# Folding the squares of an attention norm in half before the product with ones

## The chip, the cores and the metric

The kernel runs on one NeuronCore of a Trainium2 chip. The metric is the time of one execution in microseconds (us) on the device. The engines are called as the profile calls them: PE (TensorE, matrix products), DVE (VectorE), ACT (ScalarE), POOL (GpSimd) and SP (SyncE, which issues most DMA transfers).

## What the kernel computes

One layer of a hybrid decoder, on x of 1024 positions by 1024 features in float32. Eight heads of differential attention and four heads of gated linear attention (GLA) read the same normed input, and their outputs go through one output projection.

```python
h = rms_norm(x, pre_g)
z = h @ w_in                          # split into qa, ka, va, ga, qb, kb, vb, gb, gk_low
oa = diff_attention(qa, ka, va, lam)  # 8 heads, 2 softmax maps each, v of 128 features
oa = rms_norm(oa, subln_g) * (1.0 - lam_init)   # over the 128 features of a head
oa = oa * silu(ga)
ob = rms_norm(gla_chunked(qb, kb, vb, log_a), gla_g) * silu(gb)
y = concatenate([oa, ob]) @ w_out
return x + rms_norm(y, post_g)
```

The change touches only the norm of `oa`: for each head and position, the mean of the squares of 128 features.

## The kernel before

**Stages.** The input projection and GLA take the first two thirds of the span. From about 655 us to 940 us of the profile the kernel runs attention, and beside it the part of the output projection whose inputs exist already. The end of the output projection and the last norm follow.

**Exact products.** PE multiplies in a rounded 32-bit type (fp32r). Operands that need more precision are split in a high part (an ACT copy that rounds) and a low part (a DVE subtraction of the rounded value from the full one), and products are made of both. Names that end in `_hi` and `_lo` are such pairs: `wt_hi`/`wt_lo` (transposed attention weights), `m_hi`/`m_lo` (mixed values, read back from DRAM as `m_raw`), `wo_hi`/`wo_lo` (output weights).

**The streams of the attention stage.** Three generators are interleaved by `merge`, which picks the stream whose clock is behind and advances that clock by the cost that the stream yields:

- `all_scores`: for each head, eight blocks of 128 queries, from block 7 (1024 keys) down to block 0. PE makes `sc`; DVE (L1167) masks and takes the row minimum; ACT (L1177) takes exp; then DVE's reciprocal (L1202), POOL's scaling of the second map, `p1` (L1203), and DVE's subtraction of the maps into `p0` (L1207).
- `all_values`: for each head, four pairs of query blocks. Each step (`turn`) transposes three or four 128x128 blocks of `p0` on PE (`wtr`), ACT copies them to `wt_hi` (L1244), DVE makes `wt_lo` (L1245), and PE multiplies with v into `po`. ACT copies `po` to the head's output `o` (L1272), 128 features on the partitions by 512 positions.
- `out_early`: partial products of the output projection, `ypart`, three products per 128 rows of `w_out`; ACT copies them out (`yst`). The `m_hi` and `m_lo` of the attention heads come from `mix_part` (L1360, L1361), whose `m_raw` is loaded from the DRAM tensor `mixd` once enough heads are stored there. `early_ends` goes on with this around the end of the last head; the products there are `yps`.

**The norm.** `attn_norm(h, half, o)` is a generator too, and runs once for each head and half of the positions, 16 times. `mingle` puts one of its steps behind each step of the value products: half 1 runs beside the values of half 0 of the same head, half 0 beside the first values of the next head. It squares `o` (`sq`, L1282), splits the squares in a high and a low part (`sq_hl`, L1284 on ACT and L1285 on DVE), and two steps later multiplies a 128x128 matrix of ones with both parts into one PSUM bank, `ms`. Each product sums over the partitions, so `ms` is the sum of squares on every partition. ACT then makes the inverse root (`r`, L1295 and L1296), DVE multiplies `o` with it (L1297), POOL multiplies the gate (L1299), and SP stores the result into `mixd` (L1301). Of the last head nothing is stored: `last_mix` keeps the product, and `last_part` (L1367, L1368) splits it for the last `yps`.

**Queues and banks.** PE's products keep the order in which the program issues them. On ACT, DVE, POOL and SP a scheduler orders the instructions when the program is built; on the chip each engine's queue then runs strictly in that order. `wtr` and `ms` take turns on two PSUM banks (the list `TR`, counted by `n_tr`), so each use waits until the use before the last has been read out. `sq` and `r` share one buffer, and there is one buffer of `sq_hl`.

Of the kernel before, what the change touches and what calls it, by code (L numbers as in the profile page):

```python
# [8 lines left out]
F32 = mybir.dt.float32  # L9
F32R = mybir.dt.float32r  # L10
AF = mybir.ActivationFunctionType
ALU = mybir.AluOpType
PSUM = bass.MemoryType.PSUM

P = 128
# [16 lines left out]
def hymba_kernel(  # L32
# [21 lines left out]
    act, dve, pool, pe, sp = nc.scalar, nc.vector, nc.gpsimd, nc.tensor, nc.sync  # L54

    def fp(t):
        return t.bitcast(F32)

    def cols(half):
        return slice(half * 512, half * 512 + 512)  # L60
# [8 lines left out]
    ones = const.tile([P, P], F32R, name="ones")  # L69
# [28 lines left out]
    def bank(i, shape, name):  # L98
        return psum.tile(shape, F32, tag=f"b{i}", name=name)
# [10 lines left out]
    def mm(*a, **k):  # L110
        tc.keep_in_program_order(pe.matmul(*a, **k))  # L111
# [637 lines left out]
    up, keep = ku[:, 0], fp(ku)[:, 1]  # L749
# [345 lines left out]
    smp = smp_cm.__enter__()  # L1095
# [179 lines left out]
    def attn_norm(h, half, o):  # L1275
        if h < DA_HEADS - 1:
            gate = smp.tile([P, 512], F32, tag="gate", name="gate", bufs=2)
        else:
            gate = kp.tile([P, 512], F32, tag=("q1", "k1")[half], name="gate")
        sp.dma_start(gate, g_d[h][:, cols(half)])  # L1280
        sq = smp.tile([P, 512], F32, tag="r", name="sq", bufs=1)
        act.activation(sq, o, AF.Square)  # L1282
        hl = smp.tile([P, 2, 512], F32R, tag="sq_hl", name="sq_hl", bufs=1)
        act.copy(hl[:, 0], sq)  # L1284
        dve.tensor_tensor(hl[:, 1], sq, fp(hl[:, 0]), ALU.subtract)  # L1285
        yield 0.0
        yield 0.0
        n_tr[0] += 1
        ms = bank(TR[n_tr[0] % 2], [P, 512], "ms")
        for i in range(2):  # L1290
            mm(ms, ones, hl[:, i], start=(i == 0), stop=(i == 1))
        if h == DA_HEADS - 1 and not half:
            opened[TR[n_tr[0] % 2]] = None
        r = smp.tile([P, 512], F32, tag="r", name="r", bufs=1)
        act.activation(r, ms, AF.Ln, bias=eps_t, scale=1.0 / P)  # L1295
        act.activation(r, r, AF.Exp, scale=-0.5)  # L1296
        dve.scalar_tensor_tensor(r, o, sub_g, r, ALU.mult, ALU.mult)  # L1297
        dst = o if h < DA_HEADS - 1 else gate
        pool.tensor_tensor(dst, r, gate, ALU.mult)  # L1299
        if h < DA_HEADS - 1:  # L1300
            sp.dma_start(mixd[h * P : (h + 1) * P, cols(half)], o)  # L1301
            stored.append(h)
        else:
            last_mix[half] = gate
        yield 0.0
# [13 lines left out]
    def all_values():  # L1319
        carry = iter(())  # L1320
        nxt = v_first
        for h in range(DA_HEADS):
            v = nxt
            o = [smp.tile([P, 512], F32, tag="o", name="o", bufs=3) for _ in range(2)]
            yield from mingle(values(h, 3, v, o[1]), carry)
            if h + 1 < DA_HEADS:
                nxt = load_v(h + 1)
            yield from values(h, 2, v, o[1])
            yield from mingle(
                chain(values(h, 1, v, o[0]), values(h, 0, v, o[0])), attn_norm(h, 1, o[1])  # L1330
            )
            carry = attn_norm(h, 0, o[0])
        last_part(ENDS[0], parts_d[ENDS[0]])
        yield next(carry)
        yield lambda: (ENDS[2], 0) in ps_d
        early_ends()
        yield from carry
# [309 lines left out]
```

## Time and profile before

| | |
|---|---|
| Time, median of 3 runs | 977.59 us (977.15 to 982.69) |
| The profiled execution | 977.73 us |
| Its span in the profile | 976.0 us, so 1.73 us lie around it |
| PE busy | 98% of the span, 4866 products |
| DVE, ACT, POOL busy | 76%, 61%, 22% |
| Granted TensorE clock | 0.998 on average |

A row of the timeline has the start, the duration (both in us), the engine, the line of the kernel, the operation, output and inputs by the program's names, the size, and the count. In brackets stands how long the engine sat idle before it and what ended that. Matmuls are pipelined, so the durations of neighbouring ones overlap, and what one costs PE is the distance from its start to the next start.

### The profile page before, as it was taken

Reading aid. Unit: us, or ns where it says so; the run is one execution under the profiler, and the core shown is the slowest. Engines: PE = TensorE matmul, PEld = TensorE weight load, DVE = VectorE, ACT = ScalarE, POOL = GpSimd, SP = SyncE. Lnnn points to the kernel's source line nnn. Section 1 sums busy time; section 2 is a strip of 40 time slices with the busy share of each in tenths; the row PEclk is TensorE's granted clock in tenths of the full one; section 3 lists DMA queues with packets and bytes.
Section 4 is the critical chain, followed back from the end, with each engine's and each line's share of the span. In section 5 each row is a group of like instructions: output and inputs, shape, how many; then the busy total and the mean of one; then the engine's idle time right before and its main releaser. Section 6 shows DMA issues by size and latency. Waiting matters only on the chain.

```text
span 976.0 us, 14803 instructions
## 1 busy us (share of the span) xinstructions
PE 956.0 (98%) x4866; PEld 806.1 (83%) x4866; DVE 738.7 (76%) x1450; ACT 590.9 (61%) x1152; POOL 211.5 (22%) x289
## 2 busy tenths in 40 slices
PE   6999999999999999999999999999999999999997
PEld 4888888878888888888888888788888888888875
DVE  6996476889889776778787766577787778887655
ACT  8641232347467467766677774357667667787764
POOL 5420100011211221112110000023232233443232
PEclk9999999999999999999999999999999999999999
DMA  8354643768865875899986569997575678995657
GB/s 306 99 152 153 212 134 98 217 174 270 265 240 194 268 250 192 265 280 304 315 278 183 180 204 346 376 337 233 164 252 185 189 267 246 331 262 104 194 157 156
DMA packets 144556, 220.37 MB, mean 226 GB/s; under 512 B 14704, under 2 KB 78704, under 8 KB 144384
## 3 DMA queue, kind: packets, MB, share of 16 engines
q1 hardware_dynamic: 130144, 175.38, 56.6%
q0 software_dynamic: 14336, 44.05, 15.1%
q8 instruction: 38, 0.62, 0.3%
q14 instruction: 38, 0.31, 0.1%
HBM read 133.93 MB, written 88.60 MB: 228 GB/s over the span
## 4 chain that ended last, share of the span: by engine, by line
PE 86%; DMA 6%; DVE 3%; ACT 3%; issue 1%; SPq 1%; DVEq 0%; POOL 0%; ACTq 0%
PE v L111 15%; PE x L111 15%; PE ypart L111 11%; PE y L111 10%; PE z L111 10%; PE sc L111 6%; PE po L111 5%; PE yps L111 4%; PE wtr L114 3%; PE gpo L111 2%; PE kv L111 1%; DMA m_raw<-mixd 1%; DMA m_lo<-mixe 1%; DMA mixd<-o 1%; DMA k_d<-qk_st 1%
## 5 line engine op out<-in xcount | busy, mean ns | idle before, releaser
L1177 ACT ACTIVATE p<-p,stt 128x896 f32<-128x896 f32 (+7 forms) x128 | 99.3, 777 | 46.7 <-DVE stt L1167 43.5
L335 DVE TENSOR_TENSOR w<-w_raw,w 128x512 fp32r<-128x512 f32 x134 | 91.9, 690 | 32.5 <-ACT w L333 32.1
L333 ACT CAST w<-w_raw 128x512 fp32r<-128x512 f32 x134 | 82.5, 620 | 42.9 <-PE y L111 19.9
L1203 POOL TENSOR_SCALAR p<-p,stt,lam 128x1024 f32<-128x1024 f32 (+3 forms) x64 | 55.7, 871 | 209.6 <-DVE stt L1202 203.9
L1167 DVE CUSTOM_DVE_ANT_0 p<-sc,maskt 128x512 f32<-128x512 f32 (+3 forms) x128 | 74.4, 585 | 33.2 <-PE sc L111 32.5
L111 PE MATMUL y<-h_hi,w 128*128 128x512 f32 x320 | 80.6, 394 | 0.0
L111 PE MATMUL x<-s_hi,w 128*128 128x512 f32 x320 | 80.5, 394 | 0.0
L111 PE MATMUL z<-s_hi,w 128*128 128x512 f32 x320 | 80.4, 393 | 0.0
L111 PE MATMUL ypart<-wo_hi,m_hi 128*128 128x512 f32 x192 | 79.5, 414 | 0.6 <-ACT yst L1384 0.5
L111 PE MATMUL v<-w,s_hi 128*128 128x512 f32 x256 | 79.0, 389 | 0.1
L111 PE MATMUL ypart<-wo_hi,m_lo 128*128 128x512 f32 x192 | 75.6, 394 | 0.7 <-DMA m_lo<-mixe 0.7
L111 PE MATMUL ypart<-wo_lo,m_hi 128*128 128x512 f32 x192 | 75.6, 394 | 0.5 <-DMA wo_lo<-wo_d 0.5
L488 ACT COPY s<-x 128x512 f32<-128x512 f32 x60 | 35.0, 584 | 65.2 <-PE x L111 65.0
L111 PE MATMUL sc<-k,q 128*128 128x512 f32 (+1 forms) x192 | 70.9, 372 | 0.4 <-DVE stt L1167 0.4
L111 PEld LDWEIGHTS z<-s_hi,w 128*128 128x128 f32 x320 | 59.1, 188 | 11.6
L111 PEld LDWEIGHTS x<-s_hi,w 128*128 128x128 f32 x320 | 59.1, 188 | 11.7
L111 PEld LDWEIGHTS y<-h_hi,w 128*128 128x128 f32 x320 | 59.0, 188 | 11.6
L111 PE MATMUL sc<-k,qs 128*128 128x512 f32 (+1 forms) x192 | 66.6, 349 | 0.0
L285 ACT CAST w<-w_block 128x1024 fp32r<-128x1024 f32 x24 | 25.0, 1051 | 65.3 <-PE v L111 42.3
L257 DVE TENSOR_TENSOR w_raw<-w_raw 128x512 f32<-128x512 f32 x80 | 55.3, 691 | 9.6 <-DMA w_raw<-in_w_in_dram 8.6
L111 PE MATMUL v<-w,h_hi 128*128 128x512 f32 x192 | 60.0, 400 | 0.4 <-ACT h_hi L582 0.4
L1207 DVE SCALAR_TENSOR_TENSOR p<-p,stt,p 128x1024 f32<-128x1024 f32 (+3 forms) x64 | 52.3, 819 | 6.7 <-POOL p L1203 6.5
(233 smaller groups left out, 2379.8 us busy)
## 6 DMA issues: line engine op xcount, KB each, us to landing
w_raw<-in_w_in_dram SPq DMA_DIRECT2D x40, 512.0 KB, 4.9
w_block<-in_w_in_dram SPq DMA_DIRECT2D x16, 512.0 KB, 4.4
wo_raw<-in_w_out_dram POOLq DMA_DIRECT2D x32, 256.0 KB, 4.2
wo_d<-wo_hi POOLq DMA_DIRECT2D x32, 256.0 KB, 4.5
wo_d<-wo_raw POOLq DMA_DIRECT2D x32, 256.0 KB, 5.0
qs<-q_d SPq DMA_DIRECT2D x32, 256.0 KB, 8.6
k<-k_d SPq DMA_DIRECT2D x16, 512.0 KB, 9.2
q<-q_d SPq DMA_DIRECT2D x16, 512.0 KB, 7.1
```

Source lines behind the costliest of these rows:

```text
L111: tc.keep_in_program_order(pe.matmul(*a, **k))
L114: tc.keep_in_program_order(pe.transpose(dst, src, ident))
L257: dve.tensor_tensor(dst, a, b, ALU.subtract)
L285: act.copy(w[0], src)
L333: act.copy(w[0], src)
L335: split_last[:] = [dve.tensor_tensor(w[1], src, fp(w[0]), ALU.subtract)]
L488: act.copy(b[k], ps)
L1167: ins = dve.tensor_tensor_reduce(p[:, a:e], sc[:, : e - a], maskt[:, NZ + P - (e - a) :] if last else maskt[:, : e - a], 1.0, 3e38 if i == ...
L1177: act.activation(p[:, :n], p[:, :n], AF.Exp, bias=st[:, m : m + 1], scale=-1.0, accum_out=st[:, 2 + m : 3 + m],)
L1203: pool.tensor_scalar(p1[:, :n], p1[:, :n], st[:, 5:6], lam, ALU.mult, ALU.mult)
L1207: dve.scalar_tensor_tensor(p0[:, :n], p0[:, :n], st[:, 4:5], p1[:, :n], ALU.mult, ALU.subtract)
```

## The change

The upper 64 partitions of the squares are copied down beside the lower 64 (`sq_up`, on ACT), and GpSimd adds the two (L1286 of the changed kernel). Two more yields follow. The high part of the folded squares then goes to partitions 0 to 63 of `sq_hl` (L1289) and the low part to partitions 64 to 127 (L1290), and after the two yields that were there before, one product with ones sums both parts. Lines from 1285 on move down by four (L1301 becomes L1305, L1360 becomes L1364).

```diff
         sq = smp.tile([P, 512], F32, tag="r", name="sq", bufs=1)
         act.activation(sq, o, AF.Square)
-        hl = smp.tile([P, 2, 512], F32R, tag="sq_hl", name="sq_hl", bufs=1)
-        act.copy(hl[:, 0], sq)
-        dve.tensor_tensor(hl[:, 1], sq, fp(hl[:, 0]), ALU.subtract)
+        hl = smp.tile([P, 512], F32R, tag="sq_hl", name="sq_hl", bufs=1)
+        up = smp.tile([P, 512], F32, tag="sq_up", name="sq_up", bufs=1)
+        act.copy(up[:64], sq[64:])
+        pool.tensor_tensor(sq[:64], sq[:64], up[:64], ALU.add)
+        yield 0.0
+        yield 0.0
+        act.copy(hl[:64], sq[:64])
+        dve.tensor_tensor(hl[64:], sq[:64], fp(hl[:64]), ALU.subtract)
         yield 0.0
         yield 0.0
         n_tr[0] += 1
         ms = bank(TR[n_tr[0] % 2], [P, 512], "ms")
-        for i in range(2):
-            mm(ms, ones, hl[:, i], start=(i == 0), stop=(i == 1))
+        mm(ms, ones, hl, start=True, stop=True)
```

On PE nothing but `ms` moves: 16 pairs of products go, and 16 single ones appear two value steps later. This is PE's order around the norm of half 0 of head 0; `wtr` are the transposes, first of four blocks (p_6292 and p_6197 are two query blocks' weights), then of three, and `sc` the scores of the next head.

```order
 L111 MATMUL ypart<-wo_lo,m_hi 128x512
-L111 MATMUL ms<-sq_hl,ones 128x512 x2
 L114 MATMUL wtr<-ident,p_6292 128x128
 L114 MATMUL wtr<-ident,p_6197 128x128
...
 L111 MATMUL sc<-k_5896,q_6191 128x384
 L111 MATMUL sc<-k_5896,qs_6193 128x384
+L111 MATMUL ms<-sq_hl,ones 128x512
 L114 MATMUL wtr<-ident,p_6292 128x128
 L114 MATMUL wtr<-ident,p_6197 128x128 x2
```

The product moved from the place ahead of the turn of four transposes to that directly ahead of the turn of three. Between the two turns there is now an `ms` on the rotating banks, and ahead of both there is none.

The other engines' orders move more. This is ACT in the kernel before, at the end of head 3 and the start of head 4, where `m_hi_8089` is the first high part that `out_early` makes from stored heads.

```order
L1244 CAST wt_hi_7901<-wtr_7896 128x512
L1296 ACTIVATE r_7890<-r_7890 128x512
L1177 ACTIVATE p1_7881,stt_7879<-p1_7881,stt_7879 128x512
L1360 CAST m_hi_8089<-m_raw_7787 128x512
L1244 CAST wt_hi_7944<-wtr_7940 128x384
L1177 ACTIVATE p0_7930,stt_7929<-p0_7930,stt_7929 128x384
```

In the changed kernel the same cast is called `m_hi_8105` and stands some 20 rows later, behind the exp of 1024 keys and both copies `yst`. The rows after it are the norm of half 1 of head 4.

```order
L1177 ACTIVATE p1_8054,stt_8052<-p1_8054,stt_8052 128x1024
L1388 COPY yst_8121<-ypart_7799 128x512
L1388 COPY yst_8124<-ypart_7800 128x512
L1364 CAST m_hi_8105<-m_raw_7801 128x512
L1364 CAST m_hi_8127<-m_raw_7801 128x512
L1272 COPY o_7826<-po_8026 128x256
L1282 ACTIVATE sq_8195<-o_7826 128x512
L1285 COPY sq_up_8198<-sq_8195 64x512
L1289 CAST sq_hl_8197<-sq_8195 64x512
L1177 ACTIVATE p0_8154,stt_8153<-p0_8154,stt_8153 128x896
L1244 CAST wt_hi_8174<-wtr_8169 128x512
L1244 CAST wt_hi_8205<-wtr_8201 128x384
```

Behind the norm's cast the exp of 896 keys now stands ahead of the two casts `wt_hi`; before, one of these casts stood ahead of that exp. DVE at the same place of the changed kernel has both low parts behind the subtraction of the maps of 1024 keys; the kernel before had the first of them, `m_lo_8090`, some 30 rows earlier.

```order
L1245 TENSOR_TENSOR wt_lo_8102<-wtr_8097,wt_hi_8101 128x384
L1202 RECIPROCAL stt_8052<-stt_8052 128x2
L1207 SCALAR_TENSOR_TENSOR p0_8053<-p0_8053,stt_8052,p1_8054 128x1024
L1365 TENSOR_TENSOR m_lo_8106<-m_raw_7801,m_hi_8105 128x512
L1365 TENSOR_TENSOR m_lo_8128<-m_raw_7801,m_hi_8127 128x512
L1167 ISA p0_8154,stt_8153<-sc_8156,maskt_5832 128x512
```

On SP the loads of `m_raw` for these parts move as well: from ahead of the loads of the output weights' second, third and fourth row group to behind them.

The third place is the end of attention, the norms of head 7, again on ACT; `gate` is the finished product of half 1, and `m_hi` its high part for the last `yps`. First the kernel before.

```order
L1295 ACTIVATE r_9581<-ms_9578,eps_t_64 128x512
L1272 COPY o_9247<-po_9538 128x256
L1296 ACTIVATE r_9581<-r_9581 128x512
L1244 CAST wt_hi_9601<-wtr_9597 128x384
L1272 COPY o_9247<-po_9596 128x256
L1367 CAST m_hi_9393<-gate_9551 128x128
L1282 ACTIVATE sq_9616<-o_9247 128x512
L1284 CAST sq_hl_9618<-sq_9616 128x512
```

And the changed kernel at the same place.

```order
L1244 CAST wt_hi_9624<-wtr_9620 128x384
L1299 ACTIVATE r_9630<-ms_9628,eps_t_64 128x512
L1300 ACTIVATE r_9630<-r_9630 128x512
L1272 COPY o_9273<-po_9619 128x256
L1371 CAST m_hi_9421<-gate_9579 128x128
L1282 ACTIVATE sq_9646<-o_9273 128x512
L1285 COPY sq_up_9649<-sq_9646 64x512
L1371 CAST m_hi_9421<-gate_9579 128x128
L1503 COPY yps_9663<-yp_9556 128x512
L1371 CAST m_hi_9548<-gate_9579 128x128
L1289 CAST sq_hl_9648<-sq_9646 64x512
```

Half 1's inverse root moved behind the last `wt_hi`, and half 0's squares now go through a copy, POOL's addition, and three instructions of other work before their cast.

## Prediction

> **What bounds the kernel now.** I read first the engines' share of the span, then the stages, then what PE waits for in the attention stage.
>
> ```profile
> PE 956.0 (98%) x4866; PEld 806.1 (83%) x4866; DVE 738.7 (76%) x1450; ACT 590.9 (61%) x1152; POOL 211.5 (22%) x289
> ```
>
> ```profile
> 700.00:740.00 40.00, 39.89 (x235) 34.67 (x234) 30.38 (x82) 26.84 (x60) 11.72 (x13) 1.00 0.64 211
> 900.00:940.00 40.00, 38.63 (x216) 32.59 (x216) 22.11 (x61) 27.94 (x66) 9.83 (x12) 1.00 0.57 164
> ```
>
> ```profile
> PE po L111 <- ACT wt_hi L1244: 0.6, 1, 0.6
> PE ypart L111 <- ACT yst L1384: 0.5, 1, 0.5
> PE wtr L114 <- ACT r L1295: 0.4, 1, 0.4
> ```
>
> The second view has, for each stretch, its length and then the busy time of PE, its weight loads, DVE, ACT and POOL. PE leaves 0.11 us of 40 free at 700 to 740 while DVE has 10 us, ACT 13 and POOL 28 to spare. The third view lists the largest waits of PE between 655 and 976 us. The time is therefore PE's sum of products plus a handful of waits of half a microsecond. A product less is worth its whole price; a wait that appears on PE costs its whole length, however idle the engine behind it is on average. So the question is not whether ACT and POOL have time for the fold, but whether anything in PE's fixed order now comes late.
>
> **What goes.** Sixteen products with ones. At head 0's half 1 the pair stands in the stream like this:
>
> ```profile
> 705.65 0.63 PE L111 MATMUL ms<-sq_hl,ones 128*128 128x512 f32 x2
> 706.12 0.57 PE L111 MATMUL po<-wt_hi,v 128*128 128x256 f32 x4
> ```
>
> From the start of the pair to the next start are 0.47 us, so one product is 0.235 us, and 16 are **-3.8 us** (0.4%). That is all the change can give, and it is already less than the 1% that a measurement of this kernel can tell from no change.
>
> **What is added.** The price of each operation:
>
> ```profile
> L1284 ACT CAST sq_hl<-sq x16: 619/620/624, 662.0 to 934.0; 128x512 fp32r<-128x512 f32 x16
> L1285 DVE TENSOR_TENSOR sq_hl<-sq,sq_hl x16: 679/686/767, 663.8 to 934.6; 128x512 fp32r<-128x512 f32 x16
> L971 ACT COPY sq<-sq x8: 618/619/620, 374.7 to 574.2; 64x512 f32<-64x512 f32 x8
> L972 DVE TENSOR_TENSOR sq<-sq x8: 675/684/685, 375.4 to 574.9; 64x512 f32<-64x512 f32 x8
> L1299 POOL TENSOR_TENSOR o<-r,gate x14: 1282/1300/2131, 670.9 to 913.6; 128x512 f32<-128x512 f32 x14
> ```
>
> GLA's norm (L971, L972) makes the same fold and shows that 64 partitions cost what 128 cost: 619 against 620 ns on ACT, 684 against 686 on DVE. So the cast and the subtraction become no shorter, and each norm adds 0.62 us on ACT for the copy and an addition on POOL. POOL's addition of 64 partitions isn't in the trace. Its bounds are half of L1299 (0.65) and L1299's longest (2.13); I take the median, 1.30, since the other two engines show no gain from fewer partitions. From squares to `ms` the chain grows from 0.62 + 0.69 to 0.62 + 1.30 + 0.62 + 0.69, that is by 1.9 us and two handovers. Two value steps later is 3.4 us at the next place shown (718.12 to 721.5), so in most places the chain is covered; on the engines' totals (16 × 0.62 on ACT, 16 × 1.30 on POOL, over 280 us) it would be free. [...]
>
> **What is moved**, in order of time. Places where PE's order meets something late:
>
> *Half 0 of heads 0 to 3.* The product now stands directly ahead of the turn of three transposes, on the bank between the two turns' own.
>
> ```profile
> 718.12 0.62 PE L111 MATMUL ms<-sq_hl,ones 128*128 128x512 f32 x2
> 721.09 0.68 DVE L1245 TENSOR_TENSOR wt_lo<-wtr,wt_hi 128x512 fp32r<-128x512 f32 x1
> 721.94 0.49 PE L114 MATMUL wtr<-ident,p 128*128 128x128 f32 x3
> ```
>
> Before, the turn of three took the bank of `ms`, long read out. Now it takes the bank of the turn of four, free only when `wt_lo` ends, at 721.77. PE, without the pair, arrives with the single product at 721.47 and at the transposes at 721.7. That is no slack at all, with a POOL addition ahead of this block's scaling that pushes DVE's work on. I take 0.2 us for each of the four (0 to 0.7): **+0.8**.
>
> *Site A, 809 to 814 us.* The first `m_hi` and `m_lo` from stored heads are needed at 811.19 and 811.52. Before, they were made 12 us ahead. After, their loads are queued on SP behind three loads of output weights, and both casts stand on ACT behind the two copies `yst`, both subtractions on DVE behind L1207 of 1024 keys.
>
> ```profile
> 798.75 0.62 ACT L1360 CAST m_hi<-m_raw 128x512 fp32r<-128x512 f32 x1 [2.26 <-issue]
> 799.40 0.69 DVE L1361 TENSOR_TENSOR m_lo<-m_raw,m_hi 128x512 fp32r<-128x512 f32 x1 [1.87 <-ACT m_hi L1360]
> ...
> 809.42 1.15 ACT L1177 ACTIVATE p<-p,stt 128x1024 f32<-128x1024 f32 x1
> 810.57 1.05 ACT L1384 COPY yst<-ypart 128x512 f32<-128x512 f32 x2
> 810.96 1.20 POOL L1203 TENSOR_SCALAR p<-p,stt,lam 128x1024 f32<-128x1024 f32 x1 [4.81 <-DVE stt L1202]
> 811.19 0.50 PE L111 MATMUL ypart<-wo_hi,m_hi 128*128 128x512 f32 x1 [0.45 <-ACT yst L1384]
> 811.52 0.39 PE L111 MATMUL ypart<-wo_hi,m_lo 128*128 128x512 f32 x1
> 812.19 1.28 DVE L1207 SCALAR_TENSOR_TENSOR p<-p,stt,p 128x1024 f32<-128x1024 f32 x1 [1.33 <-POOL p L1203]
> ```
>
> Exp, scaling and L1207 all hang on scores that PE made before this point, so PE's wait doesn't delay them: L1207 ends at 813.47, `m_lo` 0.69 later at 814.16. PE wanted it at 811.52: **+2.6** (1.9 if DVE's chain runs 0.7 earlier against PE than it did, 3.8 with an `m_lo` as slow as the 1.91 us shown under the rivals). It is the surest of the stalls.
>
> *Right behind it*, ACT has head 4's squares, copy and cast, the cast waiting for POOL in place, and then the exp of 896 keys ahead of `wt_hi`:
>
> ```profile
> 814.82 0.59 ACT L1244 CAST wt_hi<-wtr 128x512 fp32r<-128x512 f32 x1 [0.31 <-PE wtr L114]
> 815.86 1.05 ACT L1177 ACTIVATE p<-p,stt 128x896 f32<-128x896 f32 x1 [0.46 <-DVE stt L1167]
> 817.16 0.63 PE L111 MATMUL po<-wt_hi,v 128*128 128x256 f32 x4
> ```
>
> Shifted by 2.6, `po` is due at 819.8. The copy of `o` can begin at 815.4; then 0.37, 0.63, 0.62, POOL 1.30, the cast 0.62 and the exp 1.24 with its read, so `wt_hi` runs from about 820.2 to 820.8: **+1.0** (0 to 1.6).
>
> *Half 0 of head 4.* POOL's addition is ahead of its scaling of 640 keys, and DVE makes `sq_hl`'s low part behind L1207 and behind the scores of 384 keys.
>
> ```profile
> 831.86 0.87 POOL L1203 TENSOR_SCALAR p<-p,stt,lam 128x640 f32<-128x640 f32 x1 [0.59 <-DVE stt L1202]
> 835.51 0.54 DVE L1167 CUSTOM_DVE_ANT_0 p<-sc,maskt 128x384 f32<-128x384 f32 x1
> 835.76 0.49 PE L114 MATMUL wtr<-ident,p 128*128 128x128 f32 x3
> ```
>
> The addition takes POOL until about 833.0, L1207 then ends at 834.8, L1167 at 836.05, the subtraction at 836.7; PE wants `ms` at 835.5. **+1.2** (0 to 1.6). Half 0 of head 5 has the same pattern with other sizes; I take less than half, **+0.5** (0 to 0.8).
>
> *Stores of head 6.* The last heads' parts go through DRAM.
>
> ```profile
> 900.40 0.37 SPq L1301 DMA_DIRECT2D mixd<-o  x1
> 903.72 0.90 SPq L1348 DMA_DIRECT2D m_raw<-mixd  x2
> 909.26 0.93 ACT L1469 CAST m_hi<-m_raw 128x384 fp32r<-128x384 f32 x2 [2.50 <-DMA m_raw<-mixd]
> ```
>
> ACT already waits 2.50 us for them. The norm is two steps later, so I put the store 1.7 us later and `m_raw` with it; the changed order gives ACT about 1 us of other work first: **+0.7** (0 to 1.7).
>
> *The tail.*
>
> ```profile
> 931.58 0.68 PE L111 MATMUL po<-wt_hi,v 128*128 128x256 f32 x4 [0.57 <-ACT wt_hi L1244]
> 931.80 1.29 POOL L1299 TENSOR_TENSOR gate<-r,gate 128x512 f32<-128x512 f32 x1 [10.32 <-PE wtr L114]
> 933.13 0.30 ACT L1367 CAST m_hi<-gate 128x128 fp32r<-128x128 f32 x1
> 937.56 0.62 PE L111 MATMUL ms<-sq_hl,ones 128*128 128x512 f32 x2
> ```
>
> Half 1's product now fills the wait at 931.58, but its inverse root comes behind the last `wt_hi`, so POOL's gate ends at about 934.5 and not 933.1, and ACT waits for it ahead of half 0's squares. From there: 0.29, squares until 935.5, copy 936.1, POOL 937.4, cast 938.0, subtraction 938.7. PE's last `ms` is ready at 938.7 instead of 937.56, and nothing else is left to do: **+1.4** together with the two products already counted as saved (0 to 1.9).
>
> **Sum.** 0.8 + 2.6 + 1.0 + 1.2 + 0.5 + 0.7 + 1.4 = 8.2, less 3.8: +4.4 us on the profiled execution's 977.73 (span 976.0 and 1.73 around it), 982.1; its time is within 0.2 us of the median, so **982**. All low ends give 977.7 - 3.8 + 1.9 = 975.8, all high ends 988.1.
>
> **Rivals.**
> - *Nothing waits.* The 16 products go and the scheduler's order is slack enough everywhere: 977.7 - 3.8 = 973.9, faster. For it: the averages, DVE 76%. Against: site A is read off the order and L1207's row.
> - *Only site A waits*, and PE's stall there lets the other engines run ahead so that the later places are covered: 977.7 - 3.8 + 3.6 = 977.5. For it: before, the view of PE's waits lists no more than five in 320 us. Against: the tail has nothing to run ahead of.
> - *POOL's addition is slow and everything compounds*: slower. This pair shows what POOL and DVE do to each other:
>
> ```profile
> 824.56 1.67 POOL L1299 TENSOR_TENSOR o<-r,gate 128x512 f32<-128x512 f32 x1
> 824.87 1.91 DVE L1361 TENSOR_TENSOR m_lo<-m_raw,m_hi 128x512 fp32r<-128x512 f32 x1 [0.89 <-ACT m_hi L1360]
> ```
>
>  Side by side they take 1.67 and 1.91 us, against 1.30 and 0.69 apart. At 2.1 us each addition would lengthen four exposed chains (behind site A, heads 4 and 5, tail) by 0.8 and the four early turns of three by as much: 982.1 + 8 × 0.8 = 988.5. It decides from about 1.7 us in the median. [...]
>
> **Chances.** The forecast (979.5 to 985) 0.48; only site A (976.5 to 979.5) 0.2; nothing waits 0.12; slow additions (985 to 991) 0.2. Range 975 to 988, which leaves out most of the third and a third of the last. Slower by over 1% is 987.4 and more, half of the last case: 0.1. Faster by over 1% would need 9.8 us, and only 3.8 are there: 0.01. Within: 0.89.
>
> **What would show it.** In the changed profile PE should list new waits: `ypart` on DVE's `m_lo` of over 2 us near 808 to 815, `po` on `wt_hi` of about 1 behind it, `ms` on `sq_hl` at head 4's half 0 and in the tail, `wtr` on `wt_lo` four times; 16 single `ms`; POOL's L1286 near 1.3 us. I am wrong if the wait at site A is under 1.5 us, if L1286 takes under 1 or over 1.7 us, or if the store of head 6 isn't later.

## The result and the profile after

| | before | changed |
|---|---|---|
| Median | 979.54 us (977.15 to 982.69, 6 runs) | 989.15 us (987.77 to 991.15, 6 runs) |
| Ratio | 1 | 1.0098, 95% interval 1.0072 to 1.0123 |
| Profiled execution, span | 977.73, 976.0 us | 988.76, 987.0 us |

The change makes the kernel about 9.6 us slower. The forecast was 982, that is 4.4 us slower, and the range ended at 988: the sign was as forecast, the size was too small, and the time lies outside the range.

PE does 16 products less and is busy for a smaller share of a longer span:

```profile
span 987.0 us, 14802 instructions
...
PE 957.7 (97%) x4850; PEld 805.5 (82%) x4850; DVE 746.2 (76%) x1450; ACT 599.8 (61%) x1168; POOL 232.5 (24%) x305
```

PE's waits from 655 us on, five of 0.2 to 0.6 us before, are now 19 in eleven groups; the largest groups (total, times, longest):

```profile
PE ms L111 <- DVE sq_hl L1290: 3.0, 3, 1.4
PE ypart L111 <- ACT m_hi L1364: 2.7, 1, 2.7
PE po L111 <- DVE wt_lo L1245: 2.0, 3, 1.2
PE sc L111 <- DVE stt L1167: 1.5, 2, 1.0
PE wtr L114 <- DVE wt_lo L1245: 0.9, 3, 0.4
PE yps L111 <- DVE m_lo L1372: 0.7, 1, 0.7
```

All eleven add up to 12.5 us against 2.1 before, so they more than eat the 3.8 us that the products give. To see where, I compared the two traces place by place. PE's order is the same but for `ms`, so each turn of transposes can be paired with the same turn before; the difference of their starts grows by what the stretch in between lost. The columns end at the turns that start, before the change, at 808.1, 816.1, 828.1, 853.7, 891.3 and 920.6 us, the last at the last product. They begin at 664.3, where the difference is -1.5 us in the changed kernel's profile and between -1.5 and +5.2 in all others: that much the earlier stages vary between profiled executions, whatever the kernel, and it is taken off.

| us against before | heads 0-3 | site A | behind it | head 4 half 0 | head 5 | head 6 | tail | sum | time, ratio |
|---|---|---|---|---|---|---|---|---|---|
| changed kernel | 0.1 | 5.7 | 1.2 | 1.8 | 1.0 | 1.4 | 1.3 | 12.5 | 1.0098 |
| yields only | -1.1 | 0.3 | 0.0 | -0.1 | 0.3 | 2.9 | 0.4 | 2.7 | 1.0031 |
| fold, no yields | -2.6 | -0.2 | 0.2 | 4.1 | 3.9 | -1.0 | 1.2 | 5.5 | 1.0079 |
| fold on DVE | -2.9 | 2.5 | 1.5 | 1.7 | 0.7 | 1.6 | 0.7 | 5.8 | 1.0078 |
| m_raw first | 0.2 | -0.7 | -0.1 | 5.4 | 1.0 | 2.4 | 1.2 | 9.3 | 1.0078 |
| filler | 0.1 | 2.5 | -0.2 | 1.3 | 1.0 | 0.6 | 1.3 | 6.7 | 1.0064 |
| half 1 only | -0.6 | 2.5 | -0.2 | 1.4 | 0.9 | -0.6 | 0.8 | 4.1 | 1.0054 |
| half 0 only | -1.2 | -0.7 | 0.6 | 0.1 | 1.0 | 1.8 | -0.2 | 1.3 | 1.0017 |
| own sq | -2.2 | 4.0 | 1.8 | 1.2 | 0.1 | 2.1 | 0.8 | 7.9 | 1.0083 |
| own sq, DVE | -1.9 | 4.0 | 1.2 | 0.3 | 0.3 | 1.4 | 0.2 | 5.5 | 1.0065 |
| mixed | -3.1 | -0.2 | 0.2 | 0.5 | 0.9 | 1.6 | -0.2 | -0.3 | 1.0005 |
| mixed, DVE | -1.4 | -0.2 | -0.1 | -0.3 | -0.1 | 2.2 | -0.5 | -0.5 | 0.9994 |
| one product | -2.1 | -0.2 | -0.3 | 0.0 | -0.4 | 1.1 | -0.5 | -2.4 | 0.9978 |
| rounded squares | -3.2 | -0.2 | 0.2 | -0.3 | -0.5 | 3.0 | -0.5 | -1.4 | 0.9987 |

The sums and the measured ratios (0.001 is 1 us) agree within some 3 us, so the table can be used to place the loss; single entries of less than half a microsecond are not used. One product was run in two sets; its row, and the rows of its trace further down, are those of the second.

Some entries hold a stretch in which PE's granted clock was halved. At site A in the changed kernel it was 0.50 from 812.4 to 819.3 us; products of 128x512 started 0.43 us apart there (815.91 to 816.34) and 0.23 behind it (819.65 to 819.88). They also started 0.43 us apart in the stretches at head 6 of mixed, mixed, DVE and rounded squares. The price given in brackets, and wherever a halved clock has one of 1.7 or 3.4 us, is an estimate from the granted clock, half of the stretch's length; the distances of the products give 1.6 and 3.2. The entries are: site A in the changed kernel (3.4), in own sq and in own sq, DVE (1.7 each); heads 4 and 5 in fold, no yields (1.7 each); head 4 and head 6 in m_raw first (1.7 each); head 6 in own sq, mixed, mixed, DVE and rounded squares (1.7 each).

### The profile page after: what moved, and what is told of

The parts are those of the page before. It is cut to its first block, busy times and chain, and to the rows that moved or that the text cites. A ratio compares the mean times of both kernels' runs of the same rounds, so it can differ in the third digit from the quotient of the medians.

```text
span 987.0 us, 14802 instructions
## 1 busy us (share of the span) xinstructions
PE 957.7 (97%) x4850; PEld 805.5 (82%) x4850; DVE 746.2 (76%) x1450; ACT 599.8 (61%) x1168; POOL 232.5 (24%) x305
## 4 chain that ended last, share of the span: by engine, by line
PE 86%; DVE 4%; issue 3%; ACT 3%; DMA 2%; POOL 1%; SPq 1%; DVEq 0%; ACTq 0%; POOLq 0%
PE x L111 17%; PE v L111 15%; PE y L111 11%; PE z L111 11%; PE ypart L111 9%; PE sc L111 5%; PE po L111 4%; PE yps L111 4%; PE gpo L111 3%; PE wtr L114 2%; PE kv L111 1%; DVE p L1207 1%; DMA m_lo<-mixe 1%; PE gkl_ps L111 1%; DVE p L1167 1%
## 5 line engine op out<-in xcount | busy, mean ns | idle before, releaser
L1207 DVE SCALAR_TENSOR_TENSOR p<-p,stt,p 128x1024 f32<-128x1024 f32 (+3 forms) x64 | 56.0, 877 | 9.8 <-POOL p L1203 9.6
L1244 ACT CAST wt_hi<-wtr 128x512 fp32r<-128x512 f32 (+1 forms) x80 | 43.1, 539 | 28.6 <-PE wtr L114 28.4
```

Source lines behind the costliest of these rows:

```text
L1207: dve.scalar_tensor_tensor(p0[:, :n], p0[:, :n], st[:, 4:5], p1[:, :n], ALU.mult, ALU.subtract)
L1244: act.copy(hi[:, :n], pt[:, :n])
```

## What happens at the places

**Site A.** From the changed kernel's timelines of SP, ACT and PE:

```profile
802.41 1.66 SPq L1352 DMA_DIRECT2D m_raw<-mixd  x2
808.94 1.05 ACT L1388 COPY yst<-ypart 128x512 f32<-128x512 f32 x2
811.36 1.14 ACT L1364 CAST m_hi<-m_raw 128x512 fp32r<-128x512 f32 x2 [1.37 <-DMA m_raw<-mixd]
812.03 0.51 PE L111 MATMUL ypart<-wo_hi,m_hi 128*128 128x512 f32 x1 [2.71 <-ACT m_hi L1364]
812.76 0.80 PE L111 MATMUL ypart<-wo_hi,m_lo 128*128 128x512 f32 x1 [0.22 <-DVE m_lo L1365]
```

In the kernel before the loads stood at:

```profile
792.19 1.25 SPq L1348 DMA_DIRECT2D m_raw<-mixd  x2
```

The loads of `m_raw` are issued 10 us later than before, at 802.41, and the cast that waits for them starts at 811.36. ACT stands still for the last 1.37 us, PE for 2.71; before, PE waited 0.45 us at this product. And then PE runs slowly. The columns of the stretches are as in the prediction, the granted clock third from the end:

```profile
808.00:812.00 4.00, 1.32 (x9) 1.03 (x7) 1.84 (x3) 2.63 (x6) 2.27 (x3) 1.00 1.07 392
812.00:816.00 4.00, 3.75 (x12) 3.05 (x13) 1.29 (x2) 1.28 (x3) 0.00 (x0) 0.55 1.08 254
816.00:820.00 4.00, 4.00 (x15) 3.38 (x14) 2.38 (x6) 2.58 (x6) 1.27 (x1) 0.59 1.02 382
```

After the wait the mean clock is 0.55 and 0.59 over eight microseconds, that is, 0.50 for 6.8 of them, and 12 and 15 records of products stand in 4 us, against 23.5 in the mean from 700 to 740 us before the change (235 in 40).

**Behind site A**, on POOL, DVE and PE:

```profile
825.28 0.95 POOL L1443 DMA_DIRECT2D y_d<-yst  x1 [7.05 <-ACT o L1272]
825.94 1.43 POOL L1203 TENSOR_SCALAR p<-p,stt,lam 128x896 f32<-128x896 f32 x1
827.40 1.15 DVE L1207 SCALAR_TENSOR_TENSOR p<-p,stt,p 128x896 f32<-128x896 f32 x1 [3.15 <-POOL p L1203]
830.09 0.45 PE L111 MATMUL po<-wt_lo,v 128*128 128x256 f32 x2 [1.21 <-DVE wt_lo L1245]
```

In the kernel before:

```profile
819.11 1.09 POOL L1203 TENSOR_SCALAR p<-p,stt,lam 128x896 f32<-128x896 f32 x1 [5.88 <-DVE stt L1202]
823.92 0.96 POOL L1439 DMA_DIRECT2D y_d<-yst  x1 [3.72 <-ACT p L1177]
```

An accumulating store, `y_d`, now stands ahead of the scaling of 896 keys on POOL, behind it before. POOL waits 7.05 us at the store, the scaling waits behind it, DVE waits 3.15 us at L1207, and `wt_lo` is queued behind that. What the store itself waited for the trace doesn't settle (the copy it names was just done).

**Half 0 of head 4**, on POOL, ACT, DVE and PE:

```profile
834.50 1.28 POOL L1303 TENSOR_TENSOR o<-r,gate 128x512 f32<-128x512 f32 x1 [0.63 <-DVE r L1301]
835.82 0.63 ACT L1282 ACTIVATE sq<-o 128x512 f32<-128x512 f32 x1 [0.25 <-POOL o L1303]
...
839.19 1.28 POOL L1286 TENSOR_TENSOR sq<-sq,sq_up 64x512 f32<-64x512 f32 x1
839.59 1.57 DVE L1207 SCALAR_TENSOR_TENSOR p<-p,stt,p 128x640 f32<-128x640 f32 x1
841.73 0.92 DVE L1290 TENSOR_TENSOR sq_hl<-sq,sq_hl 64x512 fp32r<-64x512 f32 x1
842.79 0.47 PE L111 MATMUL ms<-sq_hl,ones 128*128 128x512 f32 x1 [1.37 <-DVE sq_hl L1290]
```

The chain is the forecast one, with two additions. The squares of half 0 begin only when POOL has finished half 1's product, since `sq` and `r` share a buffer and half 1 ends two steps later. And L1207 takes 1.57 us beside POOL's addition, where it took 0.88:

```profile
832.76 0.88 DVE L1207 SCALAR_TENSOR_TENSOR p<-p,stt,p 128x640 f32<-128x640 f32 x1 [0.49 <-POOL p L1203]
```

## The experiments

Theory P said that the new place of the product and the store is what costs, theory F that the longer chain does. Each edit is against the kernel that its expectation names.

**Yields only.**

```diff
         act.activation(sq, o, AF.Square)
+        yield 0.0
+        yield 0.0
         hl = smp.tile([P, 2, 512], F32R, tag="sq_hl", name="sq_hl", bufs=1)
```

> The kernel before with two more yields ahead of the split, no fold, still two products with ones: only the place of the norm moves, by two value steps. If the place is what costs (theory P), most of the loss stays though no chain has grown: site A waits for m_raw again, since its loads stand behind the loads of two of the output weights' row groups, the store of head 6 is later, and nothing is saved: 984 to 990 us, PE's waits in the attention stage 7 us or more. If the longer chain of copy, addition and cast is what costs (theory F), this is the kernel before: 977 to 981 us, PE's waits about 3 us.

981.75 us, ratio 1.0031 (1.0013 to 1.0049): between the two, a third of the loss. Its waits are not at site A but at head 6 (2.9 us in the table), where the parts of the last heads go through DRAM:

```profile
PE po L111 <- DVE wt_lo L1245: 1.8, 3, 1.0
PE sc L111 <- DVE stt L1167: 1.4, 1, 1.4
```

**Fold, no further yields.**

```diff
         pool.tensor_tensor(sq[:64], sq[:64], up[:64], ALU.add)
-        yield 0.0
-        yield 0.0
```

> The changed kernel without its two more yields: the fold and the single product, in the old place, so the longer chain has to fit in the old two steps. Theory P: the loads of m_raw stand ahead of the output weights as before and site A's wait of 2.7 us is gone; 16 products are saved; 976 to 981 us. Theory F: the single product waits for its operand in nearly every norm, 16 times 0.5 to 1.5 us, and the time is 987 us or more.

986.49 us, 1.0079 (1.0050 to 1.0108), near F's number, but not by F's way: heads 0 to 3 gain 2.6 us, site A costs nothing, and of the waits of `ms` the two large ones, 2.60 and 2.22 us, are at heads 4 and 5:

```profile
PE ms L111 <- DVE sq_hl L1288: 5.3, 4, 2.6
```

Behind each of the two the clock was halved (0.66 on average from 836 to 840 us, 0.79 from 880 to 884), which by the estimate above is 3.4 of the 5.5 us in this trace's sum. The longer chain costs two waits, not sixteen, and by the same estimate some two fifths of their price (3.4 of 8.0 us) is the clock's.

**Fold with VectorE's addition.**

```diff
-        pool.tensor_tensor(sq[:64], sq[:64], up[:64], ALU.add)
+        dve.tensor_tensor(sq[:64], sq[:64], up[:64], ALU.add)
```

> The changed kernel with the addition on VectorE in GpSimd's place; yields and everything else stay. If GpSimd's slower addition (1.29 us, against 0.68 us of such an addition on DVE in GLA) is what makes the chains late, 984 to 986 us: 0.6 us less in each of some five places where PE waits for sq_hl or wt_lo. Theory P: 987 to 991 us, as the changed kernel, since the loads of m_raw stand behind all the output weights here too.

985.89 us, 1.0078 (1.0052 to 1.0105). The interval overlaps the changed kernel's, so the times don't tell the two apart. The traces do at two places: heads 0 to 3 are 3.0 us better, and site A costs 2.5 and not 5.7, since the clock there stayed at 1.00. The waits of `ms` at heads 4 and 5 stay, 1.20 and 0.74 us against 1.37 and 1.33, so they are not due to GpSimd alone.

**m_raw first.**

```diff
-            if E + 6 <= e < 2 * E:
+            if E + 6 <= e < 2 * E or e < 4:
                 tc.keep_in_program_order(ins)
...
-            sp.dma_start(raw[:, :n, :], md[:, e : e + n, part * 256 : part * 256 + 256])
+            ins = sp.dma_start(raw[:, :n, :], md[:, e : e + n, part * 256 : part * 256 + 256])
+            pin(e == 0 and len(parts_m) <= 2, ins)
```

> The changed kernel with the two first loads of m_raw held in the program's order against the first output weights' loads, so that SP issues them some four loads earlier and DVE makes m_lo ahead of the subtraction of 1024 keys. Theory S (several places, each with its own late operand): the wait of 2.7 us at site A goes with the halved clock behind it, and the 1.7 us of the accumulating store that stood ahead of POOL's scaling of 896 keys, since that order changes back too; the waits for sq_hl at heads 4 and 5 and head 6's late store stay: 983 to 985 us. Rival: the wait only moves to the next late operand, m_lo or the first output weights: 988 to 990 us.

987.11 us, 1.0078 (1.0052 to 1.0105). At its two places the edit did what was expected: site A falls from 5.7 to -0.7 and the stretch behind it from 1.2 to -0.1. But 3.6 us come back at head 4 and 1.0 at head 6, so most of the 7.7 us gained was only moved, and the interval overlaps the changed kernel's:

```profile
833.02 0.59 ACT L1389 COPY yst<-ypart 128x512 f32<-128x512 f32 x1 [3.13 <-DMA y_d<-yst]
839.80 0.47 PE L111 MATMUL ms<-sq_hl,ones 128*128 128x512 f32 x1 [3.89 <-DVE sq_hl L1290]
```

ACT, now earlier, waits 3.13 us for a store to free a `yst` buffer, with head 4's squares queued behind it. PE then waits 3.89 us for `ms` and not 1.37, and behind that the clock is halved (0.61 from 840 to 844 us), which is 1.7 of the 3.6.

**Filler.**

```diff
                 ps = y_bank(st, dh, "ypart")
+                if n == 0 and dh == 0:
+                    for _ in range(10):
+                        mm(ps, ones, wo[0][0][:, :512], start=True, stop=True)
```

> The changed kernel with ten products of ones with a weight tile, 2.35 us, into the PSUM bank of the first products of site A just before them; the real products overwrite them, so the output is as before. They fill PE's wait of 2.7 us and take no other time. If the idle PE is what halved the granted clock from 812.6 to 819 us, the clock stays at 1.00 there and the time falls by the 2.7 us that this cost, to about 986 to 987 us. If the clock fell for another reason, it falls again and the time is the changed kernel's, 989 us.

986.31 us, 1.0064 (1.0040 to 1.0088), and site A costs 2.5 us and not 5.7. The clock where the products without use run, from 814.98 to 817.40 us, and behind:

```profile
812.00:816.00 4.00, 3.77 (x21) 3.06 (x20) 1.67 (x6) 3.19 (x7) 1.25 (x2) 1.00 1.06 392
816.00:820.00 4.00, 3.86 (x20) 2.98 (x19) 2.62 (x4) 1.78 (x4) 1.02 (x2) 1.00 1.07 312
820.00:824.00 4.00, 4.00 (x25) 3.49 (x24) 3.34 (x10) 3.63 (x8) 1.29 (x1) 1.00 1.04 351
```

It stays at 1.00 with PE kept busy, so at this place the idle PE is what halved it, at a price of about 3.2 us (5.7 less 2.5). The edit also moved `y_d` back behind POOL's scaling, and the stretch behind site A fell to -0.2, as with m_raw first and half 1 only; with own sq, own sq, DVE and fold on DVE, where the store stands ahead, it is 1.8, 1.2 and 1.5. So in every trace with the store ahead this place costs 1.2 us or more, and in none of the others more than 0.6.

**Half 1 only, half 0 only.** The fold and its two yields stand under `if half:` or `if not half:`; the other half has the old two products.

> The change for half 1 of each head alone; half 0 keeps its two products and two steps. The loads of m_raw stand behind all four output weights' loads here too. Theory S: site A's wait comes back (2.5 to 5 us), head 6's late store (2 us) too, no wait for sq_hl at heads 4 and 5, eight products saved (1.9 us): 982 to 985 us. Rival, that the chain of the fold costs in every norm: half of the loss, with waits for sq_hl at half 1: 984 us too, but with ms in PE's list of waits.

> The change for half 0 of each head alone. The loads of m_raw stand where they stood before. Theory S: no wait at site A; 3 us in heads 0 to 3 (POOL's addition ahead of the scaling of 640 keys), 1.8 us each at heads 4 and 5 where ms waits for sq_hl, about 1 us in the tail, eight products saved: 982 to 985 us, PE's list led by ms waiting for sq_hl. If site A and the store of head 6, both half 1's, are nearly all of the loss: 978 to 980 us.

Half 1 only: 984.70 us, 1.0054 (1.0037 to 1.0071); half 0 only: 980.56 us, 1.0017 (1.0000 to 1.0034). The two losses add up to 7 of the 9.6 us. Half 1 brings site A, half 0 does not, as theory S has it. Half 0 is better than expected: it doesn't lose 3 us in heads 0 to 3 but gains 1.2. With half 1 in its old steps, half 0's fold is on time; so the late chain at half 0 comes from half 1's delay. And half 1 only has 1.4 us at head 4's half 0, where nothing is folded, with waits of `ms` of 0.72 and 0.25 us.

**Own sq.**

```diff
-        sq = smp.tile([P, 512], F32, tag="r", name="sq", bufs=1)
+        sq = smp.tile([P, 512], F32, tag="sq", name="sq", bufs=1)
         act.activation(sq, o, AF.Square)
-        hl = smp.tile([P, 512], F32R, tag="sq_hl", name="sq_hl", bufs=1)
+        hl = smp.tile([P, 512], F32R, tag="r", name="sq_hl", bufs=1)
```

> The changed kernel with a buffer of its own for sq; sq_hl takes the buffer that sq shared with r. Loads of m_raw and the accumulating store stand as in the changed kernel. Before, half 0's squares had to wait for POOL's product of half 1, which the change makes two steps later. If that shared buffer is what makes ms wait at heads 4 and 5 (1.4 and 1.3 us), those waits fall under 0.5 us and the time to 985 to 987 us. If DVE's order is what holds the subtraction (behind the maps of 640 keys and the scores of 384), the waits stay within 0.3 us of what they were, and so does the time, 988 to 990 us.

> Own buffer for sq and the addition on VectorE together, the rest as the changed kernel. If the places are independent, it has the gain of DVE's addition in heads 0 to 3 (3 us in the traces) and that of the own buffer: 982 to 985 us, with site A's wait for m_raw and head 6's store left. If the two only share one cause, it is not better than the better of both, 985 to 986 us.

987.75 us, 1.0083 (1.0053 to 1.0114), and with VectorE's addition 985.10, 1.0065 (1.0041 to 1.0089). In own sq `ms` has gone from PE's waits altogether:

```profile
PE po L111 <- DVE wt_lo L1245: 2.9, 5, 1.0
PE ypart L111 <- ACT m_hi L1364: 2.6, 1, 2.6
```

Heads 0 to 3 are 2.3 us better, heads 4 and 5 together 1.5. So the shared buffer is what made `ms` late. In heads 0 to 3 it isn't the only way out, since fold on DVE gains 3.0 us there with the buffer shared: late start and slow addition are both needed for that loss. The time moved by less than the intervals tell: part came back as waits of `po` for `wt_lo`, and site A kept its wait.

**Mixed.** Own sq, and the further yields for half 0 alone:

```diff
         pool.tensor_tensor(sq[:64], sq[:64], up[:64], ALU.add)
-        yield 0.0
-        yield 0.0
+        if not half:
+            yield 0.0
+            yield 0.0
```

> The fold in all 16 norms with GpSimd's addition, sq in a buffer of its own, and the two more yields for half 0 alone; half 1 keeps its old two steps. The loads of m_raw and the accumulating stores then stand as in the kernel before, and half 0's squares wait for nobody. If the loss is the sum of those places and not the fold's own operations, the time is 976 to 980 us: 16 products saved (3.8 us) less some waits that remain at heads 4 to 6. If the longer chain itself costs, as with the fold and no further yields (7.7 us), 984 us or more.

> The same with VectorE's addition. If GpSimd's addition still delays the scaling of 640 keys and its neighbours, this is 1 to 2 us faster than with GpSimd; if the places were all, the two are the same within 0.5 us.

978.71 us, 1.0005 (0.9984 to 1.0025), and 978.00 with VectorE, 0.9994 (0.9977 to 1.0010). All 16 folds are there, and the loss is gone. So is the gain of 3.8 us: heads 4 to 6 take back 3.0 in the first trace and 1.8 in the second, 1.7 of it in each a halved clock at head 6. The largest of PE's waits left in the first:

```profile
PE wtr L114 <- DVE wt_lo L1245: 1.9, 1, 1.9
PE wtr L114 <- DVE stt L1202: 0.8, 1, 0.8
```

GpSimd and VectorE can't be told apart here. Whether `sq` needs its own buffer once half 1 keeps its steps was not run; half 0 only, with the buffer shared, had no wait of `ms`.

**One product, and rounded squares.** The first multiplies with the high part alone; the second has ACT write the squares in the rounded type.

```diff
-        for i in range(2):
-            mm(ms, ones, hl[:, i], start=(i == 0), stop=(i == 1))
+        mm(ms, ones, hl[:, 0], start=True, stop=True)
```

> The kernel before with one product of the high part alone; the low part of the squares is left out, so the sum is rounded. It measures what 16 products are worth where the order hardly moves. Both theories: 3.8 us under the kernel before, about 975 to 976 us where that has 979. If a product in this stream is worth less than the distance to the next start, the time is the same as before.

> The same kernel as one_product, whose profiled execution was disturbed: the kernel before with one product of the high part, the low part of the squares left out. Its trace should show every pair replaced by 0.235 us less, about 3.7 us between 655 and 976 us, and PE's waits as before, at 974 to 976 us in all.

> The kernel before with the squares written by ACT in the rounded type at once: no cast, no subtraction, no addition, one product; the low part of the squares is left out. It tells what a cheaper norm is worth when no chain grows. 16 products are 3.8 us, and 10 us of ACT and 11 us of DVE go besides. If only PE's products count, 975 to 976 us as with one product of the high part; if the shorter chain also takes waits off PE, 973 to 974.5 us.

One product: 975.09 us, 0.9966 (0.9948 to 0.9984), and again 976.00, 0.9978 (0.9962 to 0.9994). Rounded squares: 976.81, 0.9987 (0.9967 to 1.0007). The trace of the first gains until head 6 and gives back 1.1 us there, rounded squares 3.0, of which the halved clock is 1.7. In one product's trace:

```profile
906.77 0.93 ACT L1468 CAST m_hi<-m_raw 128x384 fp32r<-128x384 f32 x2 [4.04 <-DMA m_raw<-mixd]
907.60 0.58 ACT L1498 COPY yps<-yp 128x512 f32<-128x512 f32 x1
908.12 0.82 ACT L1177 ACTIVATE p<-p,stt 128x640 f32<-128x640 f32 x1
909.66 0.55 PE L114 MATMUL wtr<-ident,p 128*128 128x128 f32 x3 [2.05 <-ACT r L1294]
```

Before, ACT waited 2.50 us here and PE 0.40. The casts start 2.5 us earlier than before (909.26), nearly as much as PE gained. But the copy `yps` and the exp of 640 keys, which stood ahead of the casts before, stand behind them now, and the inverse root that PE waits for stands behind those. One product is the only version that beats both kernels, by 0.2 to 0.3%, and it computes less.

## Why the prediction was wrong

The way of reading was right: PE's sum and a few late operands; 3.8 us on offer, and site A, heads 4 and 5, head 6 and the tail as the places that lose. Two steps failed. The prediction took the start of half 0's chain as given, and its terms for half 0 of heads 0 to 5 are 3.0 us short; and it priced a wait at its own length, where the halved clock behind site A's wait took another 3.2 us of the profiled execution. Most other sizes were too small as well. In the changed kernel's trace, with the saved products put back and the 0.45 us taken off that PE waited at site A before:

| term | predicted | trace |
|---|---|---|
| half 0 of heads 0 to 3 | 0.8 | 2.0 |
| site A, wait | 2.6 | 2.5 |
| site A, halved clock | none | about 3.2 |
| behind it | 1.0 | 1.4 |
| half 0 of head 4 | 1.2 | 2.0 |
| head 5 | 0.5 | 1.5 |
| stores of head 6 | 0.7 | 1.9 |
| tail | 1.4 | 1.8 |
| 16 products | -3.8 | -3.8 |
| sum | 4.4 | 12.5 |

- **Products.** 0.235 us each was right: in heads 0 to 3 one product's steps are -0.18 to -0.26 per norm, 0.23 in the mean.
- **Site A.** The length was right by luck, since the last link was wrong. I let `m_lo` behind L1207 end the wait; `m_hi` did, because `m_raw` landed late, and `m_lo` added 0.22. No term had the clock: I priced a wait at its own length, and this one cost about twice that in the profiled execution.
- **Behind site A.** The sum was near, the cause another. I forecast `po` late by `wt_hi`; it was late by `wt_lo`, through a store on POOL whose new place I had in the order and did not follow.
- **Half 0.** The step that failed is the one that took the chain's start as given. I moved the end of half 1's norm by two steps, but not the buffer that half 0's squares share with it. Own sq shows that this is the cause of the `ms` waits, and heads 0 to 3 gain with it as well. I also priced L1207 at its time alone, 0.88, while the prediction's own last pair of rows showed a subtraction of DVE at 1.91 us beside POOL, against 0.69 apart.
- **Head 6.** 0.7 was too small by 1.2: ACT waits 3.81 us for `m_raw` and not 2.50. Yields only, with no fold, loses 2.9 there, and its ACT waits 3.85 us, so the later store is enough for it. It isn't the only way to lose there: half 0 only, whose half 1 is in its old place, loses 1.8.

```profile
920.45 0.51 ACT L1473 CAST m_hi<-m_raw 128x384 fp32r<-128x384 f32 x1 [3.81 <-DMA m_raw<-mixd]
```

- **POOL's addition** is 1.29 us in the median, where 1.30 was taken:

```profile
L1286 POOL TENSOR_TENSOR sq<-sq,sq_up x16: 1270/1290/1802, 661.2 to 946.0; 64x512 f32<-64x512 f32 x16
```

The rival of slow additions gave the right time, 988.5, for a wrong reason. The range's end at 988 was the sum of all high ends. Nearly all terms were short on the same side, since one delay of half 1 fed several of them.

The profiled execution lost 12.5 us after 664 us while the medians differ by 9.6. Without the halved clock it would be about 9.3. Only one execution of each kernel has a trace, but each timed run has its mean granted clock: 0.995 in the profiled one, 0.994 to 0.999 in the six. The stretch of 6.8 us takes 0.0035 off that mean, so the two runs at 0.998 and 0.999 can't have had it, and they took 989.55 and 988.12 us. So the 9.6 us of the medians hang little on the clock. What those two runs lost instead has no trace and stays open.

## What to carry to other kernels

When a step moves, follow each buffer that it holds to its next user, and each in-order queue that it reorders, before pricing the operations: here copy, addition and cast cost about the 3.8 us that the products gave, and no more, once half 1 stayed in its place and `sq` had a buffer of its own, and the same operations with a shared buffer and a later store cost 1%. The saving of 0.4% on a saturated engine was smaller than what one late operand cost it: 3.8 us against 5.7 at site A. Delays that share one cause are not independent terms, so their high ends belong together in the range.

## What the runs showed that I had not expected

A wait of PE of 2.71 us at site A was followed by a granted clock of 0.50 for 6.8 us. Behind waits of 2.56 us in own sq, 2.60 and 2.22 in fold, no yields, 1.93 in mixed, and 1.81 and 0.86 close together in own sq, DVE, the clock was halved for 3.4 us. But behind 2.53 us in half 0 only, 2.12 and 0.56 in fold on DVE, and 1.23 and 1.44 in half 1 only it stayed at 1.00.

So the length of a wait alone did not decide it: 1.93 us was followed by a halved clock and 2.53 us was not. What did decide it is not shown; no run varied the length of a wait alone.
